# Modulation weights in quarters between the token tiles, all on TensorE: the prologue of a two-layer mixer kernel

## The chip, the cores and the metric

The kernel runs on one core of a Trainium2 chip. The metric is the device time of one execution in microseconds (us). Engines are named as in the profile: PE is TensorE (PEld its weight loads), DVE is VectorE, ACT is ScalarE, POOL is GpSimd, SP is SyncE, which only issues transfers here.

## The reference, cut to what matters

Two layers run over 1024 latent tokens and 256 context tokens of width 1024. Only the start of the first layer matters here: a modulation vector is computed from the conditioning, the tokens are normalised and modulated with it, and then projected.

```python
def mixer_layer(layer_idx, x, ctx, c, c_ctx, norm_g, w_mod, b_mod, w_in, ...):
    shift, scale, gate = jnp.split(jax.nn.silu(c) @ w_mod + b_mod, 3, axis=-1)
    shift_c, scale_c, gate_c = jnp.split(jax.nn.silu(c_ctx) @ w_mod + b_mod, 3, axis=-1)
    h = rms_norm(x, norm_g) * (1 + scale[:, None]) + shift[:, None]
    hc = rms_norm(ctx, norm_g) * (1 + scale_c) + shift_c
    p = h @ w_in
    ...
    x_new = x + gate[:, None] * mixer_out(a_in, b_in, attn, g, w_fourier, w_pool, pool_scale, w_out)
```

`w_mod` is 1024 x 3072, `w_in` 1024 x 3072, all in fp32.

## The kernel before, in words

Tokens come in ten tiles of 128 (0 to 7 latent, 8 and 9 context), channels in eight tiles of 128. The tokens fall into three groups: group 0 is tiles 0 to 3, group 1 is tiles 4 to 7, group 2 is the context. A block (k, g) is channel tile k of group g. `h_block` (L273) makes it: four (or two) PE transposes of the normalised tokens, an eviction that applies scale and shift (`hf`, on DVE L286 or on ACT L284), and a split in a high part (ACT, L287) and a low part (POOL, or DVE for group 2, L289). The product of a block with the weights of the fourier gate is `gk`: for each of two halves of the weights three matmuls (high x high, low x high, high x low, L340), accumulated over the eight k into six banks, one for each half and group. The gate's matmuls of a block are recorded three items behind its `hb`.

Shift and scale of the first layer are made in quarters: quarter q gives those of channel tiles 2q and 2q + 1, from four transfers of 0.5 MB (`mod0_load`). Quarters 0 to 2 are matmuls (`mod0_mm`, L157) with the two silu columns as the stationary operand, 16 passes of 512 columns in the trace; DVE copies the row (L162), PE turns it (L166) and DVE adds the bias and forms the scale (`mod_finish`, L136 to L141). Quarter 3 is made on DVE: `mod0_acc` (L176, L178) multiplies and adds elementwise, one step an item, and `mod0_sum` (L187) sums over partitions with matmuls against ones.

Each engine executes its instructions in the order in which the code records them, so the order of the work is the order of the Python lines. In the first layer it is the list `items` with the extra work `at[n]` ahead of item n: `rms` of a token tile (squares on ACT L266, three small POOL operations L267 to L269), `norm` (DVE, L575). SP issues all transfers in order: twelve of the modulation, two of the first gate weights, ten token tiles, four of quarter 3, two of the next weights. `w_split` (L321) splits staged weights: two high parts on ACT (L317), a low part on DVE and one on POOL (L318). Small work tiles come from a pool of nine buffers; the Fourier tables (`fourier_tabs`, `fourier_load`) take seven of them until the prologue is over. Behind the prologue come the Fourier matrices (L384) and the second projection, again on L340.

Of the kernel before, what the change touches and what calls it, by code (L numbers as in the profile page):

```python
# [22 lines left out]
KT = D // 128  # L23
# [8 lines left out]
def build(tc, I, out):  # L32
# [47 lines left out]
    ones = C([128, 128], "ones")  # L80
# [4 lines left out]
    # silu(c) = 0.5 c (1 + tanh(c/2))  # L85
# [44 lines left out]
    def mod_finish(l, k, sh, scl):  # L130
        """sh, scl: [128, n, 2] products for the n channel tiles from k on"""
        n = sh.shape[1]

        def cols(t, o):
            return t[:, l, o + k:o + k + n].unsqueeze(2).to_broadcast([128, n, 2])
        dve.tensor_tensor(shiftT[l][:, k:k + n, :], sh, cols(bmodT, 0), ADD)  # L136
        t = SM(16)
        tv = t.rearrange("p (k t) -> p k t", t=2)[:, 0:n, :]
        dve.tensor_tensor(tv, scl, cols(bmodT, 8), ADD)
        dve.tensor_scalar(tv, tv, 1.0, None, ADD)  # L140
        dve.tensor_tensor(scaleT[l][:, k:k + n, :], tv, cols(ngT, 0), MULT)  # L141

    def mod0_load(q):
        """shift and scale for the channel tiles 2q and 2q + 1"""
        ws = []
        for kp in range(KT // 2):
            w = T5([128, 2, 512])
            sp.dma_start(w, I["wmS"][q, 2 * kp:2 * kp + 2].rearrange("k p c -> p k c"))
            ws.append(w)
        return ws  # L150

    def mod0_mm(ws, half_way=None):
        ps = PX()
        for k in range(KT):
            if k == KT // 2 and half_way:
                half_way()
            pe.matmul(ps[0:2, :], lhsT=sc[:, k, :], rhs=ws[k // 2][:, k % 2, :], start=(k == 0), stop=(k == KT - 1))  # L157
        return ps

    def mod0_fin(q, pm):  # L160
        row = E2()
        dve.tensor_copy(row[0:2, :], pm[0:2, :])  # L162
        ps = PX()
        psv = ps[:, 0:8].rearrange("p (i c t) -> p i c t", i=2, c=2)
        for i in range(4):
            pe.transpose(ps[:, 2 * i:2 * i + 2], row[0:2, i * 128:i * 128 + 128], ident[0:2, 0:2])  # L166
        mod_finish(0, 2 * q, psv[:, 0], psv[:, 1])

    def mod0_acc(ws, acc):
        for k in range(KT):  # L170
            for i in range(2):
                w = ws[k // 2][:, k % 2, i * 256:i * 256 + 256]
                for t in range(2):
                    a, sk = acc[:, 2 * i + t, :], sc[:, k, t:t + 1]
                    if k == 0:
                        dve.tensor_scalar(a, w, sk, None, MULT)  # L176
                    else:
                        dve.scalar_tensor_tensor(a, w, sk, a, MULT, ADD)  # L178
            yield

    def mod0_sum(q, acc):
        ps = PX()
        psv = ps[:, 0:8].rearrange("p (i c t) -> p i c t", i=2, c=2)
        for i in range(2):
            for ct in range(2):
                for t in range(2):
                    pe.matmul(psv[:, i, ct, t:t + 1], lhsT=acc[:, 2 * i + t, ct * 128:ct * 128 + 128],  # L187
                              rhs=ones[:, 0:1], start=True, stop=True)
        mod_finish(0, 2 * q, psv[:, 0], psv[:, 1])

    def mod_acc(src, c0, sides, res, eng2=None):
        """elementwise over k: acc[p, s, col] = sum_k w[k*128+p, col] * silu(c)_s[k*128+p] for 512 columns"""
        acc = T5([128, 2, 512])
        res.append(acc)
        ws = []

        def load(kp):
            w = T5([128, 2, 512])
            act.dma_start(w, src[2 * kp:2 * kp + 2, :, c0:c0 + 512].rearrange("k p c -> p k c"))
            ws.append(w)  # L200
        load(0)
        load(1)
        yield
        for k in range(KT):
            for s in sides:
                a, w, sk = acc[:, s, :], ws[k // 2][:, k % 2, :], sc[:, k, s:s + 1]
                if k == 0:
                    dve.tensor_scalar(a, w, sk, None, MULT)
                else:
                    dve.scalar_tensor_tensor(a, w, sk, a, MULT, ADD)  # L210
            if k % 2 and k // 2 + 2 < KT // 2:
                load(k // 2 + 2)
            yield
# [45 lines left out]
    def x_rms(x, r):  # L259
        """r = 1 / rms of the rows of x"""  # L260
# [65 lines left out]
    def w_get(*lo_eng):  # L326
        """the next chunk; the one after it is split and the next again loaded meanwhile"""
        w_split(*lo_eng)
        w_dma()
        return wready.pop(0)  # L330
# [20 lines left out]
    def proj_tok(H, W, npair, post):  # L351
        """token-major [128 tokens, 256 columns], two token tiles to a bank"""
# [26 lines left out]
    def fourier_mix(cs):  # L379
        """[C' | -S'], [S' | C'] with C' = cos W, S' = sin W"""  # L380
# [14 lines left out]
    def fourier_fft(A, ntok):  # L395
        """8-point transform over the high digit of the token; 2-point for the context"""
# [27 lines left out]
    # F: 0 Z0, 1 Z4, (2, 3) Z1, (4, 5) Z2 and its -imaginary part, (6, 7) Z3, 8 and 9 the context's  # L424
    def fourier_chan(F, M, ntok):
        """channel transforms; frequencies k and 8 - k are sum and difference of the real and imaginary parts'"""
# [60 lines left out]
    def pooling(l, ct, wpb, gs, b, ntok):  # L487
        psc = pscT[:, l, ct:ct + 1]
        zs = []
        for c0, L in ((0, SEQ), (SEQ, CTX)):  # L490
# [17 lines left out]
            else:  # L508
                # windows of 8 replace those of 2, and of 16 those of 4
# [22 lines left out]
    def layer(l, src, dst, carry):  # L532
# [19 lines left out]
        # ---- tokens, and with them the fourier gate  # L552
# [7 lines left out]
        if full:  # L560
# [20 lines left out]
            def gk(k, *gs):  # L581
                for ct in range(2):
                    proj_T_k(psg[ct], H, W, ct, ntokA, k, gs)

            wm = [mod0_load(q) for q in range(3)]
            w_dma()
            x_in(0, 1, 2, 3, 4, 5, 6, 7, 8, 9)
            ms = [mod0_mm(wm[0])]
            ms.append(mod0_mm(wm[1], lambda: mod0_fin(0, ms[0])))
            ms.append(mod0_mm(wm[2], lambda: mod0_fin(1, ms[1])))  # L590
            w_split()
            W = wready.pop(0)
            a3 = T5([128, 4, 256])
            psg = [[PX() for _ in cols(ntokA)] for _ in range(2)]
            items = [(k, g) for g in (0, 1, 2) for k in range(6)] + [(k, g) for k in (6, 7) for g in (0, 1, 2)]
            at = {n: [] for n in range(len(items))}
            at[0] += [lambda: rms(0, 1, 2, 3), lambda: norm(0, 1), lambda: mod0_fin(2, ms[2]), lambda: norm(2, 3)]
            for n, j in enumerate((4, 5, 6, 7, 8, 9)):
                at[n] += [lambda j=j: rms(j)]
                at[n + 1] += [lambda j=j: norm(j)]  # L600
            for n in range(8, 16):
                at[n] += [lambda: next(acc)]
            at[18] += [lambda: mod0_sum(3, a3)]
            for n in range(len(items) + 3):
                if n < len(items):
                    for f in at[n]:
                        f()
                    hb(*items[n], 6 <= n < 17)
                if n == 0:
                    w3 = mod0_load(3)  # L610
                    acc = mod0_acc(w3, a3)
                    w_dma()
                if n >= 3:
                    gk(*items[n - 3])
                if n == 20:
# [4 lines left out]
                if n == 22:  # L620
                    w_split()
                    w_dma()
        else:
# [35 lines left out]
        # small tables for what follows  # L659
# [58 lines left out]
        # ---- rest of the output projection, its loads ahead of the stores of the gates  # L718
# [45 lines left out]
        # ---- k, q, v  # L764
# [17 lines left out]
        def k_late():  # L782
            """the end of a post of k, behind the start of the next"""
# [9 lines left out]
        def qk_post(qk, c):  # L793
            def post(p, bank):
# [6 lines left out]
                if qk == 0:  # L801
                    # scaled by 1/8 for the scores
# [44 lines left out]
        # k transposed: rows [hi; lo] per map  # L847
# [15 lines left out]
        # ---- attention and the rest of the output projection  # L863
# [3 lines left out]
        def q_split(u, half=0):  # L867
            """parts of q per map: [hi, lo, hi]; two heads to a tile for the context, in two halves"""
# [62 lines left out]
        def expo(u, m):  # L931
# [3 lines left out]
            if u == units[0]:  # L935
                # ahead of the release of the tokens, in a slot of the weights
# [83 lines left out]
        def z_out(u):  # L1020
            """z replaces the gate"""
# [24 lines left out]
        # columns of the output projection, and the steps from the end of the tile to each;  # L1046
        # in smaller pieces at the very end
# [23 lines left out]
        def tile_rms(j):  # L1071
            """in pieces for successive steps"""
# [42 lines left out]
        def step(i):  # L1115
# [4 lines left out]
            # tiles whose last unit was finished some iterations before  # L1120
# [62 lines left out]
        def early():  # L1183
            """the first unit, and the scores of the second, beside the last of v"""
# [172 lines left out]
```

## Time and profile before

| | before |
|---|---|
| time, median of 3 runs | 1475.15 us (1474.24 to 1475.6) |
| span of the profiled execution | 1476.5 us |
| PE busy | 94% |
| DVE busy | 67% |
| POOL busy | 52% |
| ACT busy | 39% |

The profiled execution has only its span, from the first to the last instruction, as its time; it lies 1.35 us above the median of the runs, which were not profiled. The page averages over the whole span, so it says little of the prologue. That is read from the timeline of the first 95 us and from the busy time and granted clock in stretches of 2 us. The profile's "PEclk" is the clock that TensorE was granted, as a share of 2.4 GHz: 1.00 or 0.50 (1.2 GHz), and a mean where a stretch has both.

### The profile page before, as it was taken

To read this page: it belongs to the slowest core of one execution; us is meant where nothing else is said; L and a number is where in the kernel's file an instruction comes from. 1 tells how busy PE (TensorE), PEld (TensorE's weight loads), DVE (VectorE), ACT (ScalarE), POOL (GpSimd) and SP (SyncE) were. 2 spreads that over 40 slices of the span, in tenths; PEclk is the share of its full clock that TensorE was granted. 3 is DMA by queue.
4 is the path that set the end of the run, shared out by engine and by line. 5 is a ranking of instruction groups with operands and counts; after the bars stand their busy time and mean duration, and the time that the engine had idled before them with its cause. 6 is when DMAs were issued, how large, how long until landed. Compare 5 with 4: busy or idle time off the path is not lost.

```text
span 1476.5 us, 24260 instructions
## 1 busy us (share of the span) xinstructions
PE 1391.2 (94%) x9364; PEld 1245.2 (84%) x9364; DVE 992.0 (67%) x1667; ACT 579.9 (39%) x1230; POOL 774.4 (52%) x827
## 2 busy tenths in 40 slices
PE   7899999899999988899998999999999998999998
PEld 1678899789999977888887788888999997888887
DVE  2854458876883298788988653482564249888995
ACT  2633112101323274666665342120232236565663
POOL 2543122557783066666667742245986027666663
PEclk9999999999999999999999999999999999999999
DMA  9221332673232121112113222527212111111210
GB/s 353 96 85 33 127 112 90 223 247 126 72 115 72 57 73 58 58 46 70 44 66 107 83 64 81 177 82 243 99 55 93 45 44 44 43 44 44 77 39 30
DMA packets 65155, 137.09 MB, mean 93 GB/s; under 512 B 7312, under 2 KB 19728, under 8 KB 65040
## 3 DMA queue, kind: packets, MB, share of 16 engines
q1 hardware_dynamic: 49712, 108.82, 22.1%
q10 hardware_dynamic: 15328, 26.72, 5.3%
q8 instruction: 74, 1.21, 0.4%
q14 instruction: 41, 0.34, 0.1%
HBM read 105.63 MB, written 29.88 MB: 92 GB/s over the span
## 4 chain that ended last, share of the span: by engine, by line
PE 48%; DVE 22%; issue 4%; POOL 3%; DMA 3%; ACT 2%; ACTq 0%; POOLq 0%; DVEq 0%; SPq 0%
PE x L360 18%; DVE sm L925 7%; PE x L1061 6%; PE S L915 6%; PE x L340 5%; PE x L998 5%; DVE sm L928 3%; PE x L753 3%; PE x L982 2%; DVE t L985 1%; DVE qs L882 1%; DMA xpart<-e 1%; DVE t L210 1%; PE x L894 1%; PE x L856 1%
## 5 line engine op out<-in xcount | busy, mean ns | idle before, releaser
L360 PE MATMUL x<-wh,t 128*128 128x256 f32 x2432 | 445.0, 284 | 0.0
L360 PEld LDWEIGHTS x<-wh,t 128*128 128x128 f32 x2432 | 380.7, 192 | 1.8 <-issue 1.0
L360 PE MATMUL x<-wl,t 128*128 128x256 f32 x1216 | 344.3, 283 | 1.4 <-DVE wl L318 0.9
L925 DVE TENSOR_REDUCE sm<-S 128x1 f32<-128x1280 f32 (+1 forms) x132 | 194.9, 1477 | 73.6 <-PE S L915 72.6
L360 PEld LDWEIGHTS x<-wl,t 128*128 128x128 f32 x1216 | 233.0, 192 | 3.1 <-issue 1.2
L943 ACT ACTIVATE t<-S,sm,rq 128x1280 f32<-128x1280 f32 (+1 forms) x140 | 184.5, 1321 | 24.4 <-DVE sm L928 23.4
L915 PE MATMUL S<-t,e 128*128 128x512 f32 (+1 forms) x768 | 184.4, 376 | 3.0 <-ACT e L901 1.5
L340 PE MATMUL x<-t,wh 128*128 128x512 f32 (+1 forms) x640 | 172.0, 379 | 10.1 <-DVE t L289 5.1
L998 PE MATMUL x<-t,t 128*128 128x128 f32 x1312 | 159.1, 277 | 2.3 <-DVE t L985 1.7
L998 PEld LDWEIGHTS x<-t,t 128*128 128x128 f32 x1312 | 155.6, 194 | 5.5 <-DVE t L985 2.0
L915 PEld LDWEIGHTS S<-t,e 128*128 128x128 f32 x768 | 128.7, 193 | 21.9 <-ACT t L943 2.8
L340 PEld LDWEIGHTS x<-t,wh 128*128 128x128 f32 x640 | 113.2, 190 | 33.1 <-DVE t L289 5.9
L318 POOL TENSOR_TENSOR wl<-st,wh 128x1024 fp32r<-128x1024 f32 x36 | 92.7, 2576 | 86.3 <-ACT wh L317 85.7
L317 ACT ACTIVATE wh<-st 128x1024 fp32r<-128x1024 f32 x64 | 64.8, 1058 | 138.8 <-DMA xpart<-e 45.0
L966 POOL TENSOR_TENSOR t<-t,t 128x768 f32<-128x768 f32 (+1 forms) x64 | 116.1, 1813 | 5.3
L958 POOL TENSOR_SCALAR t<-t,sm 128x768 f32<-128x768 f32 x62 | 85.6, 1381 | 51.9 <-DVE sm L954 33.2
L982 PE MATMUL x<-ident,t 128*128 128x128 f32 x636 | 102.6, 277 | 6.0 <-DVE e L1064 4.9
L1061 PE MATMUL x<-wh,e 128*128 128x512 f32 (+1 forms) x312 | 100.3, 389 | 3.9 <-ACT t L987 2.7
L753 PE MATMUL x<-wh,t 128*128 128x512 f32 x288 | 93.5, 403 | 8.9 <-DVE t L528 4.7
L340 PE MATMUL x<-t,wl 128*128 128x512 f32 (+1 forms) x320 | 99.5, 372 | 0.0
L210 DVE SCALAR_TENSOR_TENSOR t<-t,sc,t 128x512 f32<-128x512 f32 x98 | 92.2, 982 | 2.2 <-DMA t<-in_wmB_dram 1.8
L982 PEld LDWEIGHTS x<-ident,t 128*128 128x128 f32 x636 | 75.1, 142 | 17.1 <-DVE e L1064 7.5
(225 smaller groups left out, 2324.6 us busy)
## 6 DMA issues: line engine op xcount, KB each, us to landing
st<-in_w_in_dram SPq DMA_DIRECT2D x48, 512.0 KB, 4.2
t<-in_wmB_dram ACTq DMA_DIRECT2D x24, 512.0 KB, 5.4
xpart<-e ACTq DMA_DIRECT2D x36, 256.0 KB, 4.4
t<-xpart SPq DMA_DIRECT2D x18, 512.0 KB, 3.9
t<-in_wmS_dram SPq DMA_DIRECT2D x16, 512.0 KB, 9.4
st<-in_w_out_dram SPq DMA_DIRECT2D x16, 512.0 KB, 4.7
t<-in_x_dram SPq DMA_DIRECT2D x10, 512.0 KB, 10.3
e<-in_x_dram SPq DMA_DIRECT2D x20, 256.0 KB, 4.8
```

Source lines behind the costliest of these rows:

```text
L210: dve.scalar_tensor_tensor(a, w, sk, a, MULT, ADD)
L318: lo_eng[hf].tensor_tensor(lo[:, sl, :], st, hi[:, sl, :].bitcast(F32), SUB)
L340: pe.matmul(p[:, :m], lhsT=W[wi][:, k, ct * 128:ct * 128 + 128], rhs=H[k][hi][:, c0:c0 + m], start=(n == 0), stop=(n == 3 * KT - 1))
L360: pe.matmul(bank[:, i * 256:i * 256 + 256], lhsT=H[k][hi][:, j * 128:j * 128 + 128], rhs=W[wi][:, k, :], start=(n == 0), stop=(n == 3 * KT ...
L753: pe.matmul(ps, lhsT=zr[k][zi][:, j * 128:j * 128 + 128], rhs=W[wi][:, k, :], start=(n == 0), stop=(n == 11))
L915: pe.matmul(S[:, i * nk + c:i * nk + c + n], lhsT=s["qT"][i][:, m * 2 + f, :], rhs=kT[2 * h + m][:, k0 + c:k0 + c + n], start=(f == 0), st ...
L925: dve.tensor_reduce(mx, S[:, :nh * nk].rearrange("p (h k) -> p h k", h=nh), AX.X, ALU.max)
L943: act.activation(p[:, sl], S[:, sl], AF.Exp, bias=nb[:, i:i + 1], scale=rqs[:, i:i + 1], accum_out=ls[:, i:i + 1])
L966: pool.tensor_tensor(p[0][:, cut:end], p[0][:, cut:end], p[1][:, cut:end], ADD)
L982: pe.transpose(ps[:, i * 128:i * 128 + 128], s["p"][0][:, (t0 + i) * 128:(t0 + i + 1) * 128], ident)
L998: pe.matmul(o[:, i * 128:i * 128 + 128], lhsT=s["PT"][:, i * nkt + t, :], rhs=vv[h][:, kt0 + t, :], start=(t == 0), stop=(t == nkt - 1))
L1061: pe.matmul(ps[:, :m], lhsT=zz[:, k, :], rhs=Wa[hf][wi][:, k, w0:w0 + m], start=(n == 0), stop=(n == 11))
```

## The change

All four quarters are matmuls now; `mod0_acc`, `mod0_sum` and the accumulator `a3` are gone. Only two quarters are loaded ahead of the first gate weights and token tiles 0 to 7. The third follows behind those tiles, then the context's tiles, then the fourth quarter and the next weights. A number in `items` stands for a quarter: its matmuls, one outstanding gate block, and its finishing. The items start with four channel tiles of group 0, four of group 1 and quarter 2, then go on with tiles 4 and 5, the context, quarter 3, and tiles 6 and 7. The eviction goes to ACT on every second item. The gate's banks are taken when first used. The tables are loaded at item 18 (before at 20) and the next weights are split at item 20 (before at 22); items are counted with the quarters.

```diff
-    def mod0_mm(ws, half_way=None):
+    def mod0_mm(ws):
         ps = PX()
         for k in range(KT):
-            if k == KT // 2 and half_way:
-                half_way()
             pe.matmul(ps[0:2, :], lhsT=sc[:, k, :], rhs=ws[k // 2][:, k % 2, :], start=(k == 0), stop=(k == KT - 1))
-        return ps
-
-    def mod0_fin(q, pm):
         row = E2()
-        dve.tensor_copy(row[0:2, :], pm[0:2, :])
+        dve.tensor_copy(row[0:2, :], ps[0:2, :])
+        return row
+
+    def mod0_fin(q, row):
...
-    def mod0_acc(ws, acc):
...
-    def mod0_sum(q, acc):
...
-            wm = [mod0_load(q) for q in range(3)]
+            wm = [mod0_load(q) for q in range(2)]
             w_dma()
-            x_in(0, 1, 2, 3, 4, 5, 6, 7, 8, 9)
-            ms = [mod0_mm(wm[0])]
-            ms.append(mod0_mm(wm[1], lambda: mod0_fin(0, ms[0])))
-            ms.append(mod0_mm(wm[2], lambda: mod0_fin(1, ms[1])))
+            x_in(0, 1, 2, 3, 4, 5, 6, 7)
+            row = mod0_mm(wm[0])
+            row1 = mod0_mm(wm[1])
+            mod0_fin(0, row)
             w_split()
             W = wready.pop(0)
-            a3 = T5([128, 4, 256])
-            psg = [[PX() for _ in cols(ntokA)] for _ in range(2)]
-            items = [(k, g) for g in (0, 1, 2) for k in range(6)] + [(k, g) for k in (6, 7) for g in (0, 1, 2)]
+            rms(0, 1, 2, 3)
+            wm.append(mod0_load(2))
+            x_in(8, 9)
+            wm.append(mod0_load(3))
+            w_dma()
+            norm(0, 1)
+            mod0_fin(1, row1)
+            norm(2, 3)
+            items = [(k, 0) for k in range(4)] + [(k, 1) for k in range(4)] + [2]
+            items += [(k, g) for k in (4, 5) for g in (0, 1)] + [(k, 2) for k in range(6)] + [3]
+            items += [(k, g) for k in (6, 7) for g in (0, 1, 2)]
...
-            for n in range(len(items) + 3):
-                if n < len(items):
-                    for f in at[n]:
-                        f()
-                    hb(*items[n], 6 <= n < 17)
...
+            late = []
+            for n, it in enumerate(items):
+                for f in at[n]:
+                    f()
+                if isinstance(it, int):
+                    row = mod0_mm(wm[it])
+                    gk(*late.pop(0))
+                    mod0_fin(it, row)
+                    continue
+                hb(*it, n % 2 == 1)
+                late.append(it)
+                if len(late) > 3:
+                    gk(*late.pop(0))
-                if n == 20:
+                if n == 18:
...
-                if n == 22:
+                if n == 20:
                     w_split()
                     w_dma()
+            for it in late:
+                gk(*it)
```

On PE, at the first gate block, before: the end of block (0, 0), the transposes of block (4, 0) from token tiles 0 to 3 (t_17 to t_20), and the start of block (1, 0).

```order
L340 MATMUL x_231<-t_68_295,wl_222 128x512
L280 MATMUL x_399<-ident,t_17_150 128x128
L280 MATMUL x_399<-ident,t_18_152 128x128
L280 MATMUL x_399<-ident,t_19_154 128x128
L280 MATMUL x_399<-ident,t_20_156 128x128
L340 MATMUL x_228<-t_82_328,wh_221 128x512
```

The same place on PE after the change; t_17 to t_20 are token tiles 4 to 7 here, since the third quarter is no longer loaded ahead of them.

```order
L316 MATMUL x_354<-t_63_279,wl_191 128x512
L256 MATMUL x_362<-ident,t_17_150 128x128
L256 MATMUL x_362<-ident,t_18_152 128x128
L256 MATMUL x_362<-ident,t_19_154 128x128
L256 MATMUL x_362<-ident,t_20_156 128x128
L316 MATMUL x_353<-t_71_300,wh_190 128x512
```

Between the gate blocks (0, 0) and (1, 0) stood transposes of tokens that were in use already; now those of the next four tiles stand there.

On PE, at the last quarter, before: a context gate block, the sums of DVE's products against ones, and the transposes of block (6, 0).

```order
L340 MATMUL x_233<-t_90_349,wl_222 128x256
L187 MATMUL x_642<-ones,t_38_227 128x1 x8
L280 MATMUL x_658<-ident,t_17_150 128x128
```

After, at the same place:

```order
L316 MATMUL x_576<-t_79_321,wl_191 128x256
L155 MATMUL x_627<-t_51_244,sc 2x512 x2
L155 MATMUL x_627<-t_52_246,sc 2x512 x2
L155 MATMUL x_627<-t_53_248,sc 2x512 x2
L155 MATMUL x_627<-t_54_250,sc 2x512 x2
L316 MATMUL x_575<-t_87_342,wh_190 128x256
```

The eight one-column sums have become eight matmuls of 512 columns, with the next context gate block behind them.

On POOL, at the end of the prologue, before: the low parts of blocks (6, 0), (6, 1), (7, 0) and (7, 1), and then that of the next weights.

```order
L289 TENSOR_TENSOR t_145_657<-e_147_663,t_144_656 128x512
L289 TENSOR_TENSOR t_145_657<-e_149_678,t_144_656 128x512
L617 TENSOR_SCALAR pscT<-pscT 128x4
L289 TENSOR_TENSOR t_160_720<-e_162_726,t_159_719 128x512
L289 TENSOR_TENSOR t_160_720<-e_164_741,t_159_719 128x512
L318 TENSOR_TENSOR wl_752<-st_316,wh_751 128x1024
```

After:

```order
L605 TENSOR_SCALAR pscT<-pscT 128x4
L265 TENSOR_TENSOR t_153_655<-e_155_661,t_152_654 128x512
L294 TENSOR_TENSOR wl_666<-st_254,wh_665 128x1024
L265 TENSOR_TENSOR t_153_655<-e_161_680,t_152_654 128x512
L265 TENSOR_TENSOR t_165_704<-e_167_710,t_164_703 128x512
L265 TENSOR_TENSOR t_165_704<-e_169_725,t_164_703 128x512
```

The low part of the next weights has moved from behind the four low parts to behind the first of them. ACT's order has the two high parts of the same weights moved in the same way.

## Rows read from the trace of the kernel before

**Rows 1.** The page, section 4: shares of the chain that ended last, by engine.
```profile
PE 48%; DVE 22%; issue 4%; POOL 3%; DMA 3%; ACT 2%; ACTq 0%; POOLq 0%; DVEq 0%; SPq 0%
```
**Rows 2.** Stretches of 10 us: busy us (count) of PE, PEld, DVE, ACT, POOL; clock; DMA.
```profile
100.00:110.00 10.00, 10.00 (x60) 8.86 (x60) 4.52 (x11) 2.26 (x3) 3.71 (x4) 1.00 0.13 44
...
190.00:200.00 10.00, 10.00 (x70) 8.77 (x69) 2.55 (x4) 3.85 (x6) 2.40 (x1) 1.00 0.31 92
```
**Rows 3.** The same in stretches of 2 us.
```profile
30.00:32.00 2.00, 0.00 (x0) 0.00 (x0) 0.75 (x1) 1.99 (x7) 1.82 (x5) 1.00 1.04 416
...
36.00:38.00 2.00, 1.91 (x9) 1.91 (x10) 1.43 (x4) 0.55 (x2) 0.44 (x1) 0.50 1.03 386
38.00:40.00 2.00, 2.00 (x9) 1.51 (x8) 0.80 (x2) 2.00 (x7) 1.67 (x4) 0.53 1.05 388
...
74.00:76.00 2.00, 1.87 (x10) 1.79 (x10) 1.31 (x7) 0.42 (x1) 0.00 (x0) 0.50 0.50 145
...
86.00:88.00 2.00, 0.93 (x4) 0.30 (x2) 1.52 (x3) 0.42 (x1) 2.00 (x1) 1.00 0.39 106
```
**Rows 4.** Timeline to the first block: start, us, engine, line, out<-in, count [idle before <-releaser].
```profile
18.04 7.03 PE L157 MATMUL x<-t,sc 128*2 128x512 f32 x16
...
24.03 1.06 ACT L317 ACTIVATE wh<-st 128x1024 fp32r<-128x1024 f32 x1 [21.06 <-DMA st<-in_w_in_dram]
...
25.00 0.40 PE L166 MATMUL x<-ident,e 2*128 2x2 f32 x4
...
26.44 3.00 POOL L318 TENSOR_TENSOR wl<-st,wh 128x1024 fp32r<-128x1024 f32 x1 [26.01 <-ACT wh L317]
26.59 0.63 ACT L266 ACTIVATE e<-t 128x512 f32<-128x512 f32 x1 [0.23 <-DMA t<-in_x_dram]
...
29.39 0.19 POOL L267 TENSOR_TENSOR sm<-sm 128x1 f32<-128x1 f32 x1
...
33.98 0.55 POOL L269 TENSOR_TENSOR sm<-sm,mhalf 128x1 f32<-128x1 f32 x1
...
34.63 1.41 DVE L575 TENSOR_SCALAR t<-t,sm 128x1024 f32<-128x1024 f32 x2
...
36.61 0.81 DVE L286 TENSOR_SCALAR e<-x,scaleT,shiftT 128x512 f32<-128x512 f32 x1 [0.57 <-PE x L280]
```
**Rows 5.** Timeline of the gate's items.
```profile
46.29 1.75 DVE L575 TENSOR_SCALAR t<-t,sm 128x1024 f32<-128x1024 f32 x1 [1.51 <-POOL sm L269]
...
56.72 0.71 PE L340 MATMUL x<-t,wh 128*128 128x512 f32 x2
...
58.55 0.71 PE L340 MATMUL x<-t,wh 128*128 128x512 f32 x2
...
60.16 0.71 PE L340 MATMUL x<-t,wh 128*128 128x512 f32 x2
...
61.77 0.72 PE L340 MATMUL x<-t,wh 128*128 128x512 f32 x2
```
**Rows 6.** Timeline of the last quarter, to the second projection.
```profile
72.33 1.89 PE L187 MATMUL x<-ones,t 128*128 128x1 f32 x16
...
75.11 0.15 DVE L136 TENSOR_TENSOR shiftT<-x,bmodT 128x4 f32<-128x4 f32 x1
...
75.88 0.81 DVE L286 TENSOR_SCALAR e<-x,scaleT,shiftT 128x512 f32<-128x512 f32 x1
...
77.43 1.28 POOL L289 TENSOR_TENSOR t<-e,t 128x512 fp32r<-128x512 f32 x1 [15.46 <-ACT t L287]
...
82.96 2.00 ACT L317 ACTIVATE wh<-st 128x1024 fp32r<-128x1024 f32 x2
...
85.03 3.24 POOL L318 TENSOR_TENSOR wl<-st,wh 128x1024 fp32r<-128x1024 f32 x1
...
89.30 1.05 PE L384 MATMUL x<-e 128*128 128x128 f32 x8
...
91.31 0.73 PE L340 MATMUL x<-t,wh 128*128 128x512 f32 x2 [0.95 <-DVE t L390]
```

More of the change, by code (lines that the diff above doesn't have):

```diff
@@ L166, in mod0_fin @@
             pe.transpose(ps[:, 2 * i:2 * i + 2], row[0:2, i * 128:i * 128 + 128], ident[0:2, 0:2])
-        mod_finish(0, 2 * q, psv[:, 0], psv[:, 1])
-    def mod0_acc(ws, acc):
[L170 to L179, printed above, removed]
-    def mod0_sum(q, acc):
[L182 to L188, printed above, removed]
         mod_finish(0, 2 * q, psv[:, 0], psv[:, 1])
@@ L579, in hb, with gk @@
                 h_block(l, k, g, xn, H, on_act)
-            def gk(k, *gs):
+            psg = [[None] * len(cols(ntokA)) for _ in range(2)]
+            def gk(k, g):
                 for ct in range(2):
-                    proj_T_k(psg[ct], H, W, ct, ntokA, k, gs)
-            wm = [mod0_load(q) for q in range(3)]
+                    if psg[ct][g] is None:
+                        psg[ct][g] = PX()
+                for ct in range(2):
+                    proj_T_k(psg[ct], H, W, ct, ntokA, k, (g,))
@@ L596, in layer @@
+            items += [(k, g) for k in (6, 7) for g in (0, 1, 2)]
             at = {n: [] for n in range(len(items))}
-            at[0] += [lambda: rms(0, 1, 2, 3), lambda: norm(0, 1), lambda: mod0_fin(2, ms[2]), lambda: norm(2, 3)]
-            for n, j in enumerate((4, 5, 6, 7, 8, 9)):
+            for n, j in ((0, 4), (1, 5), (2, 6), (3, 7), (8, 8), (9, 9)):
                 at[n] += [lambda j=j: rms(j)]
                 at[n + 1] += [lambda j=j: norm(j)]
-            for n in range(8, 16):
-                at[n] += [lambda: next(acc)]
@@ L603, in layer @@
-            at[18] += [lambda: mod0_sum(3, a3)]
-            for n in range(len(items) + 3):
-                if n < len(items):
-                    for f in at[n]:
-                        f()
-                    hb(*items[n], 6 <= n < 17)
[L609 to L614, printed above, removed]
-                if n == 20:
+            late = []
```

## The prediction

> **What bounds the kernel now.** I read the page first, then the granted clock in steps of 2 us, then the timeline of the first 95 us, because the change touches nothing later. The chain that ended last lies for 48% on TensorE [rows 1], and from 100 to 200 us TensorE is busy in all of every 10 us (ten rows, first and last in [rows 2]). So I take a shift of the moment at which the second projection starts (91.31 us, its first matmul in [rows 6]) to reach the end unchanged: what follows is a chain of waits between engines with no time of its own, and its order of instructions is the same.
>
> The first 91 us are not such a stretch. TensorE is bound by arrivals until 29 us: 18.04 to 25.07 is one quarter of the modulation, 16 passes of 0.44 us [rows 4]. Then it waits, 2.00 us of nothing from 30 to 32 [rows 3], for the first four token tiles. From 52 us on it is dense: the gate's first matmuls of two following blocks stand 1.83 us apart (56.72, 58.55), and with a context block between them 1.61 (60.16, 61.77) [rows 5]. The difference of 0.22 is half a set of transposes, so a full set is 0.44, a full gate block (6 matmuls) 1.39 and a context gate block 0.69. It ends with waits: TensorE is busy 0.93 of 2 us at 86 [rows 3].
>
> I cut the prologue at three marks, each with the same work behind it in both kernels: A, the first block's eviction (36.61 [rows 4]); B, the start of the last quarter's part on TensorE (72.33 [rows 6]), at which in both orders 18 blocks are transposed and 15 gate blocks done; C, the second projection (91.31).
>
> **Up to A: earlier.** Four transfers of 0.5 MB leave the queue ahead of the first gate weights and the tokens. Weights at 24.03 and the first token tile at 26.59 are two transfers apart [rows 4], so 1.28 us each, 5.1 for four. ScalarE then has the second weight half at 20.2 and is done with its high part at 21.2 (1.06), GpSimd's low part takes 3.00, to 24.2; the four rms chains there ran from 29.39 to 34.53 (33.98 + 0.55), 5.14, so to 29.4. The last norm is half of the 1.41 pair: 30.1. Before, 0.57 passed from its end (36.04) to A; now A is at **30.7**. The second quarter's matmuls end at about 21.4 and its finishing lies in the wait for the tokens. Gain **5.9**; I give it 1 either way.
>
> **A to B: later.** Two things are added. First, the gate's items now change to tokens 4 to 7 after four channel tiles, not six. TensorE's order puts the transposes of those tiles right behind the first gate block, and three finished gate blocks queue behind them. The last of these tiles is normalised at 48.04 in the trace (46.29 + 1.75 [rows 5]), 11.4 after A: squares on ScalarE, rms on GpSimd and norm on VectorE take turns with the blocks. The work per item is the same in the new order, so I take 11.4 again: TensorE goes on at 42.1, with 4 sets of transposes and one gate block done. Bounds: below, 4 items at TensorE's own 1.83, as if the tiles were never late; above, one more held norm (1.75 for the usual 0.70).
> What TensorE still has to do until B is 8 full and 6 half sets of transposes (8 x 0.44 + 6 x 0.22 = 4.8), 11 full and 3 half gate blocks (15.3 + 2.1), and the third quarter, 7.0 + 0.4, which is now in the middle of the gates: 29.6. The other engines catch up under the 7 us, so I add no wait after it: the finishing chain up to the low part, 0.77 + 2.83 with [rows 6], lies beside 4.1 us of transposes and gate blocks.
> Second, the clock. After the idle time at 30 us the granted clock was 0.50 (1.2 GHz) from 36 to 38 and 0.53 to 40 [rows 3]: 4 us that did 2 us of work. The wait from about 36 to 42 comes before the long dense run here, so I charge 2.0 to that run (bounds 0 and 4). B is then 42.1 + 29.6 + 2.0 = **73.7**, or 43.0 after A in place of 35.7: **+7.3**. The waits for VectorE's 32 products of the last quarter, which the change removes, are inside the old 35.7.
>
> **B to C: later.** Before, 19.0. Now the quarter itself takes 7.0 (its weights were loaded some 30 us earlier). Behind it: context gate block 0.69, transposes 0.40 (25.00 [rows 4]), from the first finishing step to the eviction 0.77 (75.11 to 75.88), from there to the low part 1.55 (77.43). Here the change has moved the split of the next weights ahead of five of the six last blocks. ScalarE's high parts (2.00) stand ahead of the eviction of the next block, GpSimd's low part (3.24) ahead of its low part (1.28) [rows 6]. Since the tables now take seven of the nine small buffers before all six blocks, the eviction of the block after that one waits for this low part: 2.83 more (75.88 to 78.71) and 1.28 for the next. Then 1.39 + 0.69 of gates and 2.0 to C (89.30 to 91.31), and 0.4 for hand-overs. Sum **25.5**, **+6.5**. Lower bound: TensorE's own work alone, 7.0 + 12.0 + 2.0 = 21.0, +2.0, if GpSimd hid everything. Upper: the clock falls once more, below.
>
> The sum is -5.9 + 7.3 + 6.5 = **+7.9 us**. The profiled execution's span is 1476.5, 1.35 above the median of 1475.15; on the span it gives 1484.4, on the median **1483.0**.
>
> SBUF's sharing is the one price that I could have taken otherwise. The norm that ran beside GpSimd took 1.75 for 0.70 [rows 4, 5]. The Trainium skill (SBUF — State Buffer, Who interferes with whom) says that such a VectorE operation and a GpSimd one exclude each other and that the order of issue decides who waits. By that rule, the trace agrees, and if VectorE came first in the new order the 11.4 would lose about 2 and the sum would be +5.9.
>
> **Rivals.**
> 1. The clock falls in the last stretch too. For: TensorE is about half busy for some 9 us there, and after such a stretch the clock was 0.50 from 74 to 76 [rows 3]. Against: at 86 to 88 it was half busy and stayed at 1.00. Price: 3.4 us at 1.2 GHz, 1.7 lost, and as much again in the second projection if it lasts: +2.5, **1485.5**. The Trainium skill (TensorE: Matmul & The Clock Gate, A second HAM failure mode: psum-queue depth-cycling) says that frequent short pauses between groups of matmuls that cycle through banks can make the clock fall again and again. By that rule, for which the rows speak once and once against, this rival would be the forecast.
> 2. GpSimd and ScalarE get through the last split while TensorE works, and the restart costs no clock: -5.9 + 5.3 + 2.0 = +1.4, **1476.6**, no change to be told. Against: the split waits for nothing but the eviction that stands ahead of it, and that comes only after the quarter.
> 3. Faster: the order of arrival does what it says, and TensorE is never kept waiting for tokens 4 to 7. It decides at 1.83 us an item for squares, rms, norm and low part together; the trace shows 2.85 (11.4 for four). Then B is 30.7 + 25.8 (12 full and 6 half sets, 12 full and 3 half gate blocks) + 7.4 = 63.9, -8.4 against 72.33; with +2.0 behind B it is -6.4, **1468.8**, with my +6.5 it is -1.9, 1473.2.
>
> **How the numbers follow.** A change of 0.2%, 2.95 us, is about what a measurement of this kernel can tell from none. Forecast 0.58, rival 1 0.13, rival 2 0.18, rival 3 0.11. Slower: the forecast, rival 1 and a quarter of rival 2, 0.75. Same: the rest of rival 2 and a part of rival 3, 0.16. Faster: 0.09. The forecast's own range is 1479 to 1487.5 from the bounds (11.4, the clock, the last split). To leave out no more than 2 in 10, the range goes down to the middle of rival 2 and up over most of rival 1: 1476 to 1487.5.
>
> **What would show it.** Right: the first eviction near 30.7; a wait of TensorE of some 6 us from about 36, ended by the norm of token tile 7, and the clock at 0.50 at its end; the third quarter near 51 and the last near 74; behind the last, a wait for GpSimd's low part, and GpSimd busy with the weights just before; the second projection near 99. Wrong: TensorE at work without a gap from 31 us (rival 3), or the last gate block within 12 us of the last quarter (rival 2), or a first eviction later than 33, which would take away the gain. A shift at C that is not found at the end would contradict the first paragraph.

## The result, and the profile after

The changed kernel takes 1485.46 us (median of 5 runs, 1482.97 to 1489.01), the kernel before 1475.15 (5 runs, 1473.73 to 1478.85). The ratio is 1.0067, with an interval of 1.0045 to 1.009: **slower by 0.67%**. The prediction was 1483.0, in a range of 1476 to 1487.5, with a chance of 0.75 for slower.

The page of the changed kernel, section 1 and the chain by engine, which answers to [rows 1]:

```profile
span 1483.0 us, 24241 instructions
...
PE 1397.9 (94%) x9368; PEld 1246.6 (84%) x9368; DVE 970.2 (65%) x1635; ACT 580.8 (39%) x1231; POOL 772.4 (52%) x827
...
PE 48%; DVE 22%; issue 4%; POOL 3%; DMA 2%; ACT 2%; ACTq 0%; SPq 0%; POOLq 0%; DVEq 0%
```

Neither shows where 6.5 us of span (1476.5 before) went: the shares of the chain are the same but for DMA, 2% in place of 3%. The prologue must be read by itself. Its first two thirds in the timeline of the changed kernel (start, us, engine, line, out<-in, count, idle before and what ended it):

```profile
19.90 2.35 POOL L294 TENSOR_TENSOR wl<-st,wh 128x1024 fp32r<-128x1024 f32 x1 [19.47 <-ACT wh L293]
20.05 0.63 ACT L242 ACTIVATE e<-t 128x512 f32<-128x512 f32 x1 [0.23 <-DMA t<-in_x_dram]
22.22 0.18 POOL L243 TENSOR_TENSOR sm<-sm 128x1 f32<-128x1 f32 x1
...
28.16 0.55 POOL L245 TENSOR_TENSOR sm<-sm,mhalf 128x1 f32<-128x1 f32 x1
...
30.07 0.81 DVE L262 TENSOR_SCALAR e<-x,scaleT,shiftT 128x512 f32<-128x512 f32 x1 [0.57 <-PE x L256]
...
39.71 1.74 DVE L551 TENSOR_SCALAR t<-t,sm 128x1024 f32<-128x1024 f32 x1 [1.00 <-POOL sm L245]
...
41.51 0.47 PE L256 MATMUL x<-ident,t 128*128 128x128 f32 x1 [2.41 <-DVE t L551]
...
50.77 7.03 PE L155 MATMUL x<-t,sc 128*2 128x512 f32 x16
...
73.36 7.03 PE L155 MATMUL x<-t,sc 128*2 128x512 f32 x16
```

The first token tile is worked on 6.5 us sooner (26.59 in [rows 4]) and the first eviction, mark A, stands at 30.07 (before 36.61). Then TensorE waits for the norm of token tile 7, to 41.51. The third quarter is at 50.77, the last one, mark B, at 73.36 (before 72.33). The rest, to the second projection, answers to [rows 6]:

```profile
82.41 0.81 DVE L262 TENSOR_SCALAR e<-x,scaleT,shiftT 128x512 f32<-128x512 f32 x1
...
83.79 1.99 ACT L293 ACTIVATE wh<-st 128x1024 fp32r<-128x1024 f32 x2
83.96 1.28 POOL L265 TENSOR_TENSOR t<-e,t 128x512 fp32r<-128x512 f32 x1 [16.33 <-ACT t L263]
...
85.85 2.71 POOL L294 TENSOR_TENSOR wl<-st,wh 128x1024 fp32r<-128x1024 f32 x1 [0.61 <-ACT wh L293]
...
86.49 0.66 PE L256 MATMUL x<-ident,t 128*128 128x128 f32 x4 [2.07 <-ACT e L260]
...
88.52 1.46 POOL L265 TENSOR_TENSOR t<-e,t 128x512 fp32r<-128x512 f32 x1
...
90.01 0.78 ACT L260 ACTIVATE e<-x,shiftT,scaleT 128x512 f32<-128x512 f32 x1 [2.60 <-POOL t L265]
...
91.53 2.55 POOL L265 TENSOR_TENSOR t<-e,t 128x512 fp32r<-128x512 f32 x2 [1.56 <-ACT t L263]
...
94.13 0.61 PE L316 MATMUL x<-t,wh 128*128 128x512 f32 x2
...
98.21 0.74 PE L316 MATMUL x<-t,wh 128*128 128x512 f32 x2 [0.95 <-DVE t L366]
```

The second projection, mark C, starts at 98.21 (before 91.31), 6.9 us later. ScalarE's split (L293) stands ahead of the eviction for which TensorE waits 2.07 us, GpSimd's (L294) ahead of the next low part (L265), and ScalarE's next eviction waits 2.60 for that low part. The granted clock is 0.50 at 28 to 32 us, as it was at 34 to 38 before, and then falls twice more. In stretches of 2 us (length, busy us and count of PE, PEld, DVE, ACT, POOL, then the clock, DMA share, GB/s):

```profile
30.00:32.00 2.00, 2.00 (x12) 2.00 (x11) 1.47 (x2) 1.08 (x3) 0.56 (x2) 0.50 1.05 387
...
36.00:38.00 2.00, 0.00 (x0) 0.00 (x0) 1.02 (x1) 2.00 (x6) 1.83 (x4) 1.00 1.06 390
...
42.00:44.00 2.00, 2.00 (x6) 1.52 (x6) 0.81 (x1) 0.63 (x1) 0.43 (x1) 0.50 0.79 315
44.00:46.00 2.00, 2.00 (x8) 1.66 (x7) 0.00 (x0) 0.56 (x1) 0.84 (x1) 0.50 0.05 14
...
84.00:86.00 2.00, 0.42 (x4) 0.21 (x2) 1.14 (x1) 2.00 (x3) 1.39 (x2) 1.00 0.00 0
...
88.00:90.00 2.00, 2.00 (x7) 1.51 (x7) 0.84 (x1) 0.00 (x0) 1.97 (x2) 0.50 0.65 229
```

It is 1.00 again from 34 us, 0.50 (1.2 GHz) at the end of the wait for token tile 7 and behind it, and 0.50 once more behind the 2.07 us wait of the tail.

### The profile page after: what moved, and what is told of

Read it like the earlier page. It is cut to its first block, busy times and chain, and to the rows that moved or that the text cites. A ratio compares the mean times of both kernels' runs of the same rounds, so it can differ in the third digit from the quotient of the medians.

```text
span 1483.0 us, 24241 instructions
## 1 busy us (share of the span) xinstructions
PE 1397.9 (94%) x9368; PEld 1246.6 (84%) x9368; DVE 970.2 (65%) x1635; ACT 580.8 (39%) x1231; POOL 772.4 (52%) x827
## 4 chain that ended last, share of the span: by engine, by line
PE 48%; DVE 22%; issue 4%; POOL 3%; DMA 2%; ACT 2%; ACTq 0%; SPq 0%; POOLq 0%; DVEq 0%
PE x L336 18%; DVE sm L915 7%; PE x L1051 6%; PE S L905 6%; PE x L316 5%; PE x L988 5%; PE x L743 3%; DVE sm L918 3%; PE x L972 2%; DVE t L975 1%; DVE qs L872 1%; PE x L884 1%; PE x L846 1%; POOL e L749 1%; DVE t L186 1%
## 5 line engine op out<-in xcount | busy, mean ns | idle before, releaser
L915 DVE TENSOR_REDUCE sm<-S 128x1 f32<-128x1280 f32 (+1 forms) x132 | 194.9, 1476 | 73.6 <-PE S L905 72.5
L294 POOL TENSOR_TENSOR wl<-st,wh 128x1024 fp32r<-128x1024 f32 x36 | 91.6, 2545 | 81.1 <-ACT wh L293 80.6
L293 ACT ACTIVATE wh<-st 128x1024 fp32r<-128x1024 f32 x64 | 64.8, 1059 | 133.0 <-DMA xpart<-e 44.6
## 6 DMA issues: line engine op xcount, KB each, us to landing
t<-in_x_dram SPq DMA_DIRECT2D x10, 512.0 KB, 10.3
```

The costliest lines, as they stand in the source:

```text
L294: lo_eng[hf].tensor_tensor(lo[:, sl, :], st, hi[:, sl, :].bitcast(F32), SUB)
L915: dve.tensor_reduce(mx, S[:, :nh * nk].rearrange("p (h k) -> p h k", h=nh), AX.X, ALU.max)
```

## The experiments

The theory is the prediction's: the gain at the head is real, and two places give it back, the wait for tokens 4 to 7 (with the third quarter behind it, where TensorE has no time for it) and the last split, which stands ahead of the last blocks. The rivals put it down to the quarters' matmuls as such, to buffers, or to the clock. All diffs are against the changed kernel. Where the split is moved, the issue of the next weights' transfers (`w_dma`), which stands in the same branch, moves with it. Times of before beside them: 1476.42 us (first four below) and 1476.64 (last four).

### The third quarter in the gap

```diff
-            items = [(k, 0) for k in range(4)] + [(k, 1) for k in range(4)] + [2]
+            items = [(k, 0) for k in range(4)] + [2] + [(k, 1) for k in range(4)]
```

> The changed kernel with one edit: the third quarter's matmuls stand behind the four blocks of tokens 0 to 3, ahead of the first block of tokens 4 to 7, instead of behind those. Theory (TensorE waits from 34 to 41.5 us for the norms of tokens 4 to 7, and the clock falls in that wait): the 7.0 us of the quarter fill the wait at no cost, the clock stays at 1.00 from 36 to 48, the last quarter starts at about 64 in place of 73.4, the second projection at about 89 in place of 98.2, time 9 to 9.5 us below the changed kernel, about 1476, that is about the kernel before. Rival (the quarter's own weights are late, or its finishing holds up VectorE's norms): a wait inside the quarter, last quarter at 68 to 71, gain 3 to 5. Second rival (the clock falls all the same): gain 7.

Timeline of TensorE, the two quarters and mark C:

```profile
34.44 7.03 PE L155 MATMUL x<-t,sc 128*2 128x512 f32 x16
...
65.12 7.03 PE L155 MATMUL x<-t,sc 128*2 128x512 f32 x16
...
89.97 0.74 PE L316 MATMUL x<-t,wh 128*128 128x512 f32 x2 [0.95 <-DVE t L366]
```

The same 7.03 us lie in the wait. C comes 8.24 us sooner than in the changed kernel, that is the quarter and 1.2 us more. The longest wait of TensorE between 34 us and the last quarter is now 0.52, and the clock is 1.00 in each 2 us from 34 to 48. From B to C it takes 24.85 us in both. Time 1476.0, ratio to before 0.9994 (0.9981 to 1.0008). So the wait for tokens 4 to 7 was room that the changed kernel left empty.

### The gap filled with work that nobody reads

```diff
+                if n == 3:
+                    fill = PX()
+                    for k in range(KT):
+                        pe.matmul(fill[0:2, :], lhsT=sc[:, k, :], rhs=wm[2][k // 2][:, k % 2, :],
+                                  start=(k == 0), stop=(k == KT - 1))
```

> The changed kernel, and the third quarter's eight matmuls once more, into a bank that nobody reads, right behind the first gate block; they only occupy TensorE. Theory (that place is a wait of TensorE, and 2.0 to 2.2 us are lost to the lower clock behind it): though 7.0 us of matmuls are added, the time falls: clock 1.00 from 42 to 46, last quarter at 71.2 in place of 73.4, second projection at 96.0, span about 1481. Rival (the wait costs nothing in clock): no change, 98.2. Second rival (TensorE's time counts wherever it stands): later by 7, 105.

Timeline of TensorE, and one of the 2 us stretches in which the changed kernel has 0.50:

```profile
35.18 7.03 PE L606 MATMUL x<-t,sc 128*2 128x512 f32 x16
42.14 0.66 PE L256 MATMUL x<-ident,t 128*128 128x128 f32 x4
...
49.61 7.03 PE L155 MATMUL x<-t,sc 128*2 128x512 f32 x16
...
97.06 0.74 PE L316 MATMUL x<-t,wh 128*128 128x512 f32 x2 [0.95 <-DVE t L366]
...
44.00:46.00 2.00, 2.00 (x13) 1.67 (x12) 0.00 (x0) 1.61 (x3) 1.29 (x1) 1.00 0.09 29
```

This separates the clock from the moved work. TensorE goes on 0.63 us later than in the changed kernel (42.14 for 41.51), and yet reaches the third quarter 1.16 us sooner: 7.47 us in place of 9.26 for the same items. The clock is 1.00 from 36 to 48 us. So the fall of the clock behind the gap cost **at least 1.8 us** (2.0 were charged): a few transposes that the changed kernel makes inside its wait are in the 7.47 too. C comes 1.15 us sooner, where 2.2 had been expected: the 0.63 had been left out. Time 1482.99, ratio 1.0038 (1.0026 to 1.0051): 7 us of added matmuls cost nothing.

### The split four items later

```diff
-                if n == 20:
+                if n == 24:
                     w_split()
```

Item 20 is channel tile 6's first block, item 24 the last block but one, item 25 the last, channel tile 7's context block. In two expectations below the names are off: the one on the split behind the last block says token tile 7 for channel tile 7, and the one on both edits says context blocks for the blocks of tokens 0 to 7.

> The changed kernel with one edit: the next weights are split behind item 24, block (7, 1), as far behind the blocks as in the kernel before, not behind item 20. Theory (the split stands ahead of five of the last six blocks and holds GpSimd and ScalarE): the low part of (6, 1) starts at about 85.4 instead of 88.5 us, the last gate block ends 3.5 us earlier, the second projection starts at 94.7 in place of 98.2, span about 1479.5, time about 1482. Rival (the split is only moved: the second projection then waits for its weights' low part): the second projection's first matmul at 97.5 to 98.5, or a new wait for wl just behind it, and no gain. Second rival (the order of these blocks is set by TensorE, not by GpSimd): same as the changed kernel.

```profile
90.16 2.11 DVE L294 TENSOR_TENSOR wl<-st,wh 128x1024 fp32r<-128x1024 f32 x1 [1.65 <-ACT wh L293]
...
91.14 3.33 POOL L294 TENSOR_TENSOR wl<-st,wh 128x1024 fp32r<-128x1024 f32 x1
...
92.19 2.57 DVE L265 TENSOR_TENSOR t<-e,t 128x256 fp32r<-128x256 f32 x1
...
94.81 0.39 PE L316 MATMUL x<-t,wh 128*128 128x256 f32 x1 [1.94 <-DVE t L265]
...
97.51 0.74 PE L316 MATMUL x<-t,wh 128*128 128x512 f32 x2 [0.95 <-DVE t L366]
```

GpSimd's low parts are no longer late, but a new wait takes the place of the old: 1.94 us for the low part of the last context block, on VectorE. B (73.84) to C is 23.67 us, only 1.2 less than 24.85. Time 1482.85, ratio 1.0044 (1.0023 to 1.0064). The 94.7 expected for C did not come, so this edit alone does not tell what the split costs.

The three rows show how the wait comes about. VectorE's small operation took 2.57 us where it takes 0.45 in the next kernel but one, and ended at 94.76, just behind the end of GpSimd's at 94.47; GpSimd's took 3.33 for 2.45 there, while VectorE was busy with its own half up to 92.27. The Trainium skill (SBUF — State Buffer, Who interferes with whom) says that a VectorE instruction with two inputs in SBUF contends with a GpSimd one that reads SBUF, and that the order of issue decides which waits. By that rule, the trace agrees: the end times are as if each waited for the one issued ahead of it.

### The tables later as well

```diff
-                if n == 18:
+                if n == 22:
                     dve.tensor_copy(identR, ident)
...
-                if n == 20:
+                if n == 24:
                     w_split()
```

> As the run with the late split, and the Fourier tables two items later (22 in place of 18), so that the nine small buffers are not down to two when the last six blocks are evicted. Theory (the eviction of (7, 0) waits for the low part of (6, 1) because of the two buffers): its eviction no longer waits for GpSimd, GpSimd does four low parts of 1.28 back to back, and the second projection starts about 1.3 us earlier than with the late split alone, at 93.4. Rival (the buffers' wait is covered by the banks or by GpSimd itself): as the late split alone, within 0.4. Second rival: the tables now land so late that the Fourier matrices wait for them, and the second projection starts later than with the late split alone.

B (72.86) to C (96.55) is 23.69 us, as in the kernel above, with the same wait of 1.91 us; one run took 1480.34. The 93.4 expected for C did not come. With this wait in the way the run cannot show a price of the small buffers that the tables take. The next kernel speaks against one: it has the tables at 18 as the changed kernel, and TensorE waits for no eviction there for longer than 0.19 us. The buffers hold an eviction back for long only where the low part ahead of it is late, as at 90.01 in the changed kernel.

### The split behind the last block

```diff
-                if n == 20:
+                if n == 25:
                     w_split()
```

> One edit to the changed kernel: the split of the second projection's weights stands behind the last context block (the one of token tile 7, third column group) instead of behind its first. In the kernel with the split one block earlier, TensorE waited 1.94 us near the end of the stretch for the low part of the last context block, which VectorE made in 2.57 us behind 2.11 us of its half of the split. Theory (that queue is the wait): it vanishes, and the first matmul of the second projection comes 2 us earlier than there, at 95.5, and 2.7 us before the changed kernel's 98.21. Rival (the split is only moved on): the second projection now waits for its low parts, whose two halves took 2.1 and 3.3 us and begin only then, and its first matmuls come at 97.5 or later, or have a wait of 1 to 3 us on the low parts directly behind them. What would be seen in time: about 1482.5 by the theory, 1485 by the rival.

```profile
73.74 7.03 PE L155 MATMUL x<-t,sc 128*2 128x512 f32 x16
...
90.89 0.45 DVE L265 TENSOR_TENSOR t<-e,t 128x256 fp32r<-128x256 f32 x1 [2.49 <-ACT t L263]
...
91.84 1.23 DVE L294 TENSOR_TENSOR wl<-st,wh 128x1024 fp32r<-128x1024 f32 x1 [0.50 <-ACT wh L293]
...
92.83 2.45 POOL L294 TENSOR_TENSOR wl<-st,wh 128x1024 fp32r<-128x1024 f32 x1 [1.78 <-ACT wh L293]
...
95.29 0.70 PE L316 MATMUL x<-t,wh 128*128 128x512 f32 x2 [1.04 <-DVE t L366]
```

The last low part now goes ahead of the split and takes 0.45 us, and TensorE waits for neither. GpSimd's half of the weights ends at 95.28, when the second projection starts, and TensorE has no wait from there to 200 us. B (73.74) to C is **21.55 us**, 3.3 less than in the changed kernel and 0.55 above TensorE's own work as the prediction added it up (21.0). The clock is 1.00 in each 2 us from 70 to 98. Time 1480.09, ratio 1.0024 (1.0012 to 1.0036). So the place of the split cost 3.3 us in the changed kernel, the second fall of the clock included.

### The last quarter's matmuls twice

```diff
+                    if it == 3:
+                        fill = PX()
+                        for k in range(KT):
+                            pe.matmul(fill[0:2, :], lhsT=sc[:, k, :], rhs=wm[3][k // 2][:, k % 2, :],
+                                      start=(k == 0), stop=(k == KT - 1))
                     row = mod0_mm(wm[it])
```

> The changed kernel with the last quarter's eight pairs of gate matmuls issued twice, the second time into a bank that nothing reads; TensorE does 7.03 us more in the last stretch before the second projection. Theory (there TensorE is never waiting for long enough to hide them): first matmul of the second projection 7 us later, at 105.2. Rival (as in the gap behind the first gate block, where the same 7.03 us cost nothing, they are covered in part by the waits of 2.07, 2.60 and 0.95 us that stand between them and the second projection): at 100 to 102.5.

```profile
93.80 0.66 PE L256 MATMUL x<-ident,t 128*128 128x128 f32 x4 [2.07 <-ACT e L260]
...
105.49 0.73 PE L316 MATMUL x<-t,wh 128*128 128x512 f32 x2 [0.95 <-DVE t L366]
```

C is 7.28 us later than in the changed kernel; the one run took 1495.66 us, more than this shift explains, and one run cannot tell why. The wait behind the quarter is the same 2.07: the whole tail is moved on, since what follows needs the quarter's result. In the gap the same matmuls cost nothing, here all of their 7.03.

### The last quarter on VectorE again

```diff
-            items += [(k, g) for k in (4, 5) for g in (0, 1)] + [(k, 2) for k in range(6)] + [3]
+            items += [(k, g) for k in (4, 5) for g in (0, 1)] + [(k, 2) for k in range(6)]
...
+            a3 = T5([128, 4, 256])
+            acc = mod0_acc(wm[3], a3)
+            for n in range(9, 17):
+                at[n] += [lambda: next(acc)]
+            at[19] += [lambda: mod0_sum(3, a3)]
...
-                hb(*it, n % 2 == 1)
+                hb(*it, n % 2 == 1 or 9 <= n < 18)
...
-                if n == 20:
+                if n == 19:
                     w_split()
```

> The changed kernel with one part of the change undone: the last quarter's gate products are made on VectorE again, over eight blocks, and TensorE only adds them up, with the split right behind the last quarter's channels as before. Theory (on TensorE these matmuls cost their full 7.03 us less the 0.5 to 1.5 us that the sum's own matmuls take): first matmul of the second projection at about 92, 6 us before the changed kernel's 98.21, time about 1479. Rival (VectorE's products, some 32 instructions, delay the norms and high parts of the context blocks, which TensorE then waits for): first matmul at 95 to 97, with waits of 3 us or more on VectorE or GpSimd in the stretch between 45 and 85 us, time about 1483.

Timeline, and the 2 us stretch behind the waits:

```profile
67.81 4.44 DVE L176 SCALAR_TENSOR_TENSOR t<-t,sc,t 128x256 f32<-128x256 f32 x11
...
72.17 0.41 DVE L287 TENSOR_TENSOR t<-e,t 128x256 fp32r<-128x256 f32 x1
...
72.64 0.39 PE L338 MATMUL x<-t,wh 128*128 128x256 f32 x1 [2.71 <-DVE t L287]
...
77.71 3.41 PE L185 MATMUL x<-ones,t 128*128 128x1 f32 x16
...
76.00:78.00 2.00, 1.82 (x10) 1.53 (x9) 2.00 (x7) 0.00 (x0) 0.00 (x0) 0.50 0.52 170
```

C is at 97.98, 0.23 us from the changed kernel's, and the time 1483.34, ratio 1.0044 (1.0028 to 1.0059). The rival held in kind, and C came even later than its 95 to 97: eleven products stood ahead of a low part, TensorE waited 2.71 us for it, and the clock was then 0.50 from 76 to 84 us, the sum's own matmuls included (3.41 us; 1.89 in [rows 6]). The evictions of these items are on ScalarE here, as before the change. So in this order the last quarter costs as much on VectorE as on TensorE, and its place on TensorE is neither the loss nor the gain.

### Both edits together

The third quarter in the gap, and the split behind the last block (the two diffs above).

> Both edits to the changed kernel: the third quarter's gate matmuls stand between the first four context blocks and the next four, where TensorE waits for the norms of token tiles 4 to 7, and the split of the second projection's weights stands behind the last context block. Theory (the two gains are of different places and add up): first matmul of the second projection at 87.3, which is 89.97 of the kernel with the first edit alone less 2.7; time about 1473.5, 2.5 us under the kernel before. Rival (the second edit gives nothing, or its wait moves to the second projection): first matmul at 90, time about 1476, no difference to the kernel before.

```profile
35.06 7.03 PE L155 MATMUL x<-t,sc 128*2 128x512 f32 x16
...
87.34 0.70 PE L316 MATMUL x<-t,wh 128*128 128x512 f32 x2 [1.04 <-ACT t L364]
```

C is at 87.34, as forecast, 10.87 us sooner than in the changed kernel (8.24 + 2.92 apart) and 3.97 sooner than before. Time **1469.97** (1468.41 to 1471.07), ratio to before **0.9956** (0.9944 to 0.9969): this one beats both kernels, and by 3.5 us more than the 1473.5 expected, which C does not explain. TensorE is busy in all but 0.18 us from 70 to 86, and its clock is 1.00 in each 2 us from 36 to 48 and from 70 to 98.

## Why the prediction was right

It held in time, in sign and in its steps; up to A two errors of size cancelled.

| | before | predicted | measured |
|---|---|---|---|
| A, first eviction | 36.61 | 30.7 | 30.07 |
| A to TensorE going on | 11.4 to tile 7's norm | 11.4 | 11.44 |
| third quarter | | near 51 | 50.77 |
| A to B | 35.72 | 43.0 | 43.29 |
| B to C | 18.98 | 25.5 | 24.85 |
| C | 91.31 | 99.2 | 98.21 |

**Up to A.** The gain was 6.54, not 5.9, and that it came so near was in part luck. The tokens came 6.5 us sooner where four transfers of 1.28 (5.1) had been counted (in all the kernels with this order of loads their first tile is worked on between 19.89 and 20.62); why was not traced. GpSimd's low part took 2.35 for 3.00. Against that, the four rms chains took 6.49 us (22.22 to 28.71) where 5.14 had been taken over. One reading ahead of the sum was wrong, though nothing in the sum rests on it: TensorE was not bound by arrivals until 29 us, since it is busy in all of each 2 us from 6 to 28 in the kernel before, and a quarter takes it 7.03 where its four transfers take 5.1.

**A to B.** The time that the four late tiles need, taken over unchanged from [rows 5], was right to 0.1 us. So was the norm's 1.75: it took 1.74 again. The clock's term, 2.0, measured 1.8 or a little more. What the prediction had not said is that the gap is the place for the third quarter: it had sized the one (some 6 us) and the other (7.0), but not put them side by side.

**B to C.** The steps came one after the other as listed. From the low part at 83.96 (1.55 behind the eviction at 82.41, as taken) to the end of the next at 89.98 it was 6.02 us, predicted 2.00 + 3.24 + 1.28 = 6.5. From there to the end of the two after it, at 94.08, 4.10, predicted 2.83 + 1.28 = 4.1. The size was 0.65 too high, most of it GpSimd's half of the split (2.71 for 3.24). The lower bound, 21.0 if the split were hidden, is what the split behind the last block reaches within 0.55.

**The first rival** was half right. The clock did fall in the tail: 0.78, 0.50 and 0.87 in the three stretches from 86 to 92, so 0.44 + 1.00 + 0.26 = 1.7 us of TensorE's time, just the price that the rival gave it. But by the trace C came at most some 0.3 later for it: GpSimd's last low part ended at 94.08, and the second of that block's matmuls, which reads it, starts near 94.35 (the two at 94.13 take 0.61, one of them 0.39). At full clock TensorE would have waited there. From 92 on the clock was 1.00, so nothing lasted into the second projection. By the rule of the Trainium skill (TensorE: Matmul & The Clock Gate, A second HAM failure mode: psum-queue depth-cycling), which the prediction cited for it, the trace agrees that the clock can fall again, and not that the kernel's time goes with it here.

**The second rival** fell: moving the split away gains 3.3, so it was not covered. **The third** fell with the wait that ended at 41.51; its price per block, 2.85 in place of 1.83, held. Its sum was 0.45 too high: the sets and gate blocks that it names come to 25.35, not 25.8, so its times would have been 1468.3 and 1472.8.

**From C to the end.** The shift carried over: the long run of matmuls that starts at 995.75 (before 988.99), and the last matmul at 1478.97 (1472.51) come 6.8 and 6.5 later, and in the profiled executions C to the end is 1384.8 us, before 1385.2. Over the kernels of this study the shift of C and that of the time go together, though not to better than 3.4 us where there are several runs: 6.9 and 10.3 for the changed kernel, 6.7 and 6.7, 6.2 and 6.4, 5.8 and 6.6, 4.0 and 3.5, -1.3 and -0.4, -4.0 and -6.7 (medians against before's on the same chip). The two kernels with a single run have 5.2 and 3.9, and 14.2 and 19.0. The changed kernel's 10.3 has an interval of 6.6 to 13.3, in which the predicted 7.9 lies and the traces' 6.9. What the later stages add to it, up to 3.4 us here and -2.7 with both edits, was not traced to an operation and stays open.

## What to carry to other kernels

An earlier arrival gains only what the next engine can use: here the head won 6.5 us, and the tiles behind it came no faster. Cut the stretch at marks with equal work behind them, add up what each queue holds at each mark, and put independent work where TensorE waits: 7 us of matmuls were free in the gap, and cost all 7 at the end. Work for a later stage (a split of weights) goes behind the last small operation that TensorE still waits for, not merely later.

## What was not expected of the hardware

- Work that nobody reads made the kernel no slower and C 1.15 us sooner, since the clock stayed at 1.00 across the gap. The run's own expectation had this, the prediction had not.
- A VectorE operation of 0.45 us took 2.57 beside GpSimd's part of the split, and GpSimd's 2.45 became 3.33 beside VectorE's: with the split one block later the two took 0.45 and 2.45.
- In the tail of the changed kernel the clock's fall took 1.7 us from TensorE and, by the trace, at most some 0.3 from C; behind the gap a fall of the same depth cost 1.8 or more, since TensorE had work waiting.
